# The samples' last rows in four column blocks on 128 partitions, and two row tiles weighted before their norm

## The chip, the cores and the metric

The kernel runs on one core of one Trainium2 chip. The metric is the device time of one execution in microseconds (us): the median of 3 runs of the kernel before is 829.52 us, with a lowest of 829.44 and a highest of 830.91. The profile is one execution more, recorded by the hardware profiler; its own time was 829.68 us.

## What is computed

One step of a hybrid decoder layer: a matrix-memory branch (mLSTM) and a sliding-window attention branch are merged by sigmoid gates into `u`; the output projection follows, scaled by a gate that depends on the conditions `c`, is added to the input, and a final RMS norm with the weight `g_final` ends the step. There are 1024 prompt rows and 8 x 4 = 32 sample rows, each of 1024 columns. The change touches only this end:

```
def rmsnorm(x, g):
    xf = x.astype(jnp.float32)
    y = xf * lax.rsqrt(jnp.mean(xf * xf, axis=-1, keepdims=True) + NORM_EPS)
    return (y * g.astype(jnp.float32)).astype(x.dtype)
...
    u = jax.nn.sigmoid(gm) * (y_m @ w_mo) + jax.nn.sigmoid(ga) * (y_a @ w_ao)
    x = x + gate * (u @ w_o)
...
    y_prompt = rmsnorm(yp, g_final)
    y_sample = rmsnorm(ys, g_final)
```

`u @ w_o` is a product of (1024 + 32) x 1024 by 1024 x 1024 in fp32.

## The kernel before

Everything lies in one function, `body`, which builds five instruction streams: TensorE (PE), VectorE (DVE), ScalarE (ACT), GpSimd (POOL) and the DMA queue of SyncE (SP). Each stream is executed strictly in the order in which it stands; what an instruction needs from another stream it waits for by a semaphore, and everything behind it in its own stream waits too. A scheduler makes the streams out of the program's calls: with `V.on`, `S.on` and `G.on` (line 2214) the calls on DVE, ACT and POOL from there on keep the order of the program text, PE always keeps it (`mm`, line 271), but DMAs on SP (`issue`, line 260) are placed by the scheduler, unless `late` (or a call that is `paced`) ties them behind others.

Two stages matter here.

**`mem_out(d, ...)`**, the last stage before the output rows (d = 0 to 7, the loop at line 2109). PE makes the 12-product pieces named `g_w_mo`; for each piece DVE multiplies the finished accumulator into a gate tile `tgw_mo` that SP has loaded from DRAM, and POOL (for d = 6 and 7) adds that to `u_l`, the second half of `u`. The first factor of the products, `ym_h` and `ym_l`, lies in the two memory blocks "l0" and "h0" (line 1714). The accumulators of d = 7 are in the PSUM banks that the output rows use next, so the banks come free when DVE has multiplied them out.

**The output rows** (loop at line 2219). The 1024 prompt rows go in four blocks of 256 rows, `r` = `blocks_of_rows[i]`. One block is a 2 x 2 block product by seven products (`r.product(1..7)`) over the first half of the inner dimension, and plain products (`r.plain`) over the second half, each in three passes (high x high, high x low, low x high parts). The accumulators are X, Z, W and Y (`foX`, `foZ`, `foW`, `foY` in the profile). ACT copies an accumulator on (`copied`: W becomes a copy of X, Y a copy of W) and PE then goes on adding to the original, so PE waits for those copies. ACT also splits `u` into parts for the next products (tiles `u0whC`, `u0whD` and so on), and DVE subtracts to make the low parts. In the first block ACT and DVE still split the last raw weights `wop` that SP loads (`wo_p0h`, `wo_p1h`). A row tile of 128 rows is finished in these steps: DVE adds the accumulator to the residual (`add_row`), ACT squares it with a running sum (`square`, tile `sq`), DVE and ACT make the inverse root (`norm_rows`: tiles `fv`, `fw`, `fy`; ACT does the square root), DVE multiplies by it and by `g_final` (`rows_out`, one `SCALAR_TENSOR_TENSOR` for each half of 512 columns), and SP stores it.

The tiles of this stage are eight row tiles `misc[0..7]` of 128 x 1024 (`rows_l` is 0 to 3, `rows_h` 4 to 7), which lie on the two blocks "l0" and "h0" (line 2128). So no DMA may fill any of them before the last `g_w_mo` product has read `ym_l` and `ym_h`.

The **sample rows** (`sample_rows`, a generator that `aside` moves on by a step at given places) are made beside this: 16 fp32 products of 32 x 512, four at a time in the four 32-column groups of PE (`fo`), each group holding the sum over other inner tiles; so ACT and DVE add four 32-row pieces for each half, then gate, residual, two squares of 32 x 512 and two multiplications of 32 x 512 follow in the last block.

In the last block (i = 3, `nxt` is None) `norm_rows` handles three columns: row tiles 4 and 5 of the block before and the samples; then `rows_out(4)` and `rows_out(5)` (the "fifth and sixth row tile") are four DVE multiplications.

Of the kernel before, what the change touches and what calls it, by code (L numbers as in the profile page):

```python
# [10 lines left out]
F32 = mybir.dt.float32  # L11
# [9 lines left out]
D = 1024  # L21
SEQ = 1024
# [151 lines left out]
def body(tc, a):  # L174
    nc = tc.nc
    with ExitStack() as ctx:
# [1760 lines left out]

        gbD, gsD = dp.tile([1, D], F32, name="gbD"), dp.tile([NS, D], F32, name="gsD")

        def ada_gate():  # L1940
            for j in range(2):
                cj = slice(j * 512, (j + 1) * 512)
                raws = []
                for k in range(KT):
                    raws.append(ht([128, 512], f"adar_ga{j}{k}"))
                    dma(raws[-1], a["w_ada"][4 + j, :, k])
                    yield 2.0, ""
                gb = ht([128, 512], f"gb{j}")[:9]
                dma(gb, a["b_gate"][:, cj].to_broadcast((9, 512)))
                yield 5.0, "b"  # L1950
                acc = pb([128, 512], f"ada_ga{j}")
                yield from ada_products(raws, acc)
                for r in range(0, 128, 32):
                    V.tensor_tensor(gb, acc[r:r + 9], gb, op=ALU.add)
                V.tensor_scalar(gb, gb, 0.25, None, op0=ALU.mult)
                dma(gbD[:, cj], gb[0:1])
                for t in range(NT):
                    dma(gsD.rearrange("(b t) e -> b t e", t=NT)[:, t, cj], gb[1:9])
                yield 3.0, "b" if j == 0 else ""
            dma(c32, hD[:, :, SEQ:T])  # L1960
# [168 lines left out]
        misc = [t[:, i] for t in rows for i in range(4)]  # L2129
        gsb, gf = misc[0], misc[2]  # L2130
        dma(gf, a["g_final"].to_broadcast((128, D)), True)
        S.activation(gf, gf, AF.Copy, scale=-1.0)
        dma(gsb[:NS], gsD, True)

        def residual(tb, n):
            xb = misc[3 + tb % 4 if tb < 8 else 7]
            dma(xb[:n], a["x_prompt"][tb * 128:tb * 128 + 128] if tb < 8 else a["x_sample"], tb < 4)
            return xb
# [18 lines left out]
        def rows_out(tb, xb, r, by=V):  # L2157
            yo, n = (a["y_p"][tb * 128:tb * 128 + 128], 128) if tb < 8 else (a["y_s"], NS)
            for c, eng in zip(HALF[::-1], (by, V)):
                if eng is S:  # L2160
                    S.activation(xb[:n, c], xb[:n, c], AF.Copy, scale=r[:n])
                else:
                    V.scalar_tensor_tensor(xb[:n, c], xb[:n, c], r[:n], gf[:n, c], op0=ALU.mult, op1=ALU.mult)
                issue(yo[:, c], xb[:n, c], eng=nc.scalar if eng is S else None)

# [3 lines left out]
        def sample_rows():  # L2169
            raws = [misc[m][:, c] for m in (1, 7) for c in HALF]  # L2170
            acc = [po([128, 512], f"fo8_{f}") for f in range(2)]
            sums = []

            def load(f, kq):
                for j in range(4):
                    dma(raws[j], a["w_out"][(kq + j) * 128:(kq + j + 1) * 128, HALF[f]], f == kq == 0)

            def products(f, kq):
                for j in range(4):
                    mm(acc[f][32 * j:32 * j + 32], u(kq + j, SEQ, NS), raws[j], start=(kq == 0), stop=(kq > 0), share=4)  # L2180

            load(0, 0)
            yield
            for f in range(2):
                products(f, 0)
                load(f, 4)
                yield
                products(f, 4)
                sums.append(raw_tile("fo8s").rearrange("p k n -> p (k n)")[:NS])
                S.copy(sums[f], acc[f][0:32])  # L2190
                if f == 0:
                    load(1, 0)
                else:
                    xb = residual(8, NS)
                yield
                for j in (32, 64, 96):
                    V.tensor_tensor(sums[f], acc[f][j:j + 32], sums[f], op=ALU.add)
                yield
            for f in range(2):
                V.tensor_tensor(sums[f], sums[f], gsb[:NS, HALF[f]], op=ALU.mult)  # L2200
                V.tensor_tensor(xb[:NS, HALF[f]], xb[:NS, HALF[f]], sums[f], op=ALU.add)
            row8.append(xb)

        row8 = []

# [9 lines left out]
        lo, hi = HALF  # L2215
        dma(gsb[:NS], gsD)
        blocks_of_rows[0].start("p1")
        xb = ss = None
        for i, r in enumerate(blocks_of_rows):
            nxt = blocks_of_rows[i + 1] if i < 3 else None  # L2220
            aside = lambda *when: next(rows8, None) if i in when else None
            before, xb, ss = (xb, ss), [residual(2 * i + c, 128) for c in range(2)], sm([128, 6], "fss", 2)
            aside(0)
            X, Z = pg([128, 512], "foX"), pa([128, 512], "foZ")
            r.product(1, X, True)
            W = copied(X, "foW", pg, new=r if i == 0 else None)
            if i:
# [4 lines left out]
            if i:  # L2232
                square(before[0][0][:, hi], before[1][:, 1:2])
                square(before[0][1][:, lo], before[1][:, 2:3])
                if i == 3:
                    V.memset(before[1][:, 4:6], 1.0)
                    for c in range(2):
                        square(row8[0][:NS, HALF[c]], before[1][:NS, 4 + c:5 + c])
                rs = norm_rows(before[1], 2 if nxt else 3, 2)
            if not nxt:  # L2240
                for c in range(2):
                    rows_out(4 + c, before[0][c], rs[:, c:c + 1])
            r.product(2, X, False)
# [26 lines left out]
            if nxt:  # L2270
                seventh()
                nxt.start(5)
                aside(1, 2)
                r.plain(1, 1, Z, range(2, 4))
# [10 lines left out]
            else:  # L2285
                rows_out(8, row8[0], rs[:, 2:3])
                first_row()
                seventh()
                square(xb[0][:, hi], ss[:, 1:2])
# [5 lines left out]
                for f, (y, (c0, n)) in enumerate(zip(Y, parts)):  # L2295
# [3 lines left out]
                    if f:  # L2299
                        V.tensor_tensor(xb[1][:, hi], xb[1][:, hi], gf[:, hi], op=ALU.mult)  # L2300
                        half = norm_sum(ss[:, 2:4], 1, 2)
# [9 lines left out]
OUTS = {  # L2311
    "y_p": (SEQ, D), "y_s": (NS, D), "C_p": (NH, 128, 128), "n_p": (128, NH), "m_p": (1, NH),
    "k_p": (128, 128), "v_p": (128, 128), "C_s": (NH, 128, NB, 128), "n_s": (128, NH, NB), "m_s": (NH, NB),
# [4 lines left out]
def lay_out(i):  # L2318
# [15 lines left out]
                                 xt[:, :, SEQ:].reshape(128, -1), np.zeros((128, 512 - C_TRI - 28 - KT * (9 + NS)), np.float32)], 1),  # L2334
        "x_prompt": np.asarray(i["x_prompt"])[0], "x_sample": np.asarray(i["x_sample"]).reshape(NS, D),
        "b_gate": np.asarray(i["b_ada"])[:, 2 * D:],
# [30 lines left out]
def unpack(r):  # L2367
    kv = lambda t: np.ascontiguousarray(t.transpose(1, 0, 2)).reshape(1, NB, 128, 2, 64)
    f = np.ascontiguousarray
    return (  # L2370
        r["y_p"].reshape(1, SEQ, D), r["y_s"].reshape(NB, NT, D),
        r["C_p"].reshape(1, 1, NH, 128, 128), f(r["n_p"].T).reshape(1, 1, NH, 128), r["m_p"].reshape(1, 1, NH),
# [11 lines left out]
```

## Time and profile before

| What | Value |
|---|---|
| median of 3 runs | 829.52 us |
| the profiled execution, its own time | 829.68 us |
| its span, first to last instruction | 827.9 us |
| ACT busy | 419.0 us (51%) |
| DVE busy | 590.5 us (71%) |
| DMA, mean over the span | 186 GB/s |
| output rows, first PE product to last instruction | 733.09 to 827.9 us |

The profiled execution's time is 1.8 us more than its span. Times in the views are us from the start of the span. In a timeline row the first number is the start, the second the time from there to the end of the instruction (or of the merged group, whose count stands behind the x); in brackets stands the idle time of that engine before it and what ended it. Instructions of one engine overlap a little, since the next starts before the last has drained. SPq rows are the SP queue's own: the time is that of issuing a DMA, and where rows are merged, the waits between them are in it.

### The profile page before, as it was taken

To read this page: it belongs to the slowest core of one execution; us is meant where nothing else is said; L and a number is where in the kernel's file an instruction comes from. 1 tells how busy PE (TensorE), PEld (TensorE's weight loads), DVE (VectorE), ACT (ScalarE), POOL (GpSimd) and SP (SyncE) were. 2 spreads that over 40 slices of the span, in tenths; PEclk is the share of its full clock that TensorE was granted. 3 is DMA by queue.
4 is the path that set the end of the run, shared out by engine and by line. 5 is a ranking of instruction groups with operands and counts; after the bars stand their busy time and mean duration, and the time that the engine had idled before them with its cause. 6 is when DMAs were issued, how large, how long until landed. Compare 5 with 4: busy or idle time off the path is not lost.

```text
span 827.9 us, 15032 instructions
## 1 busy us (share of the span) xinstructions
PE 810.2 (98%) x5129; PEld 670.4 (81%) x5129; DVE 590.5 (71%) x1479; ACT 419.0 (51%) x1030; POOL 67.2 (8%) x128
## 2 busy tenths in 40 slices
PE   6999999999999999999999999999999999999996
PEld 3779897888787888888888878888888789987775
DVE  4899886746646456475667886897669988864776
ACT  5664365556455564545455454544446654344343
POOL 0120000000000001000001010000002104250000
PEclk9999999999999999999999999999999999999998
DMA  9994757456535415538867444454446685643532
GB/s 335 377 341 137 225 183 233 140 163 195 176 124 187 140 65 168 177 124 270 262 209 255 159 136 137 139 180 160 136 127 202 217 298 172 202 153 116 202 109 108
DMA packets 106689, 153.95 MB, mean 186 GB/s; under 512 B 20449, under 2 KB 54369, under 8 KB 106581
## 3 DMA queue, kind: packets, MB, share of 16 engines
q1 hardware_dynamic: 100964, 142.25, 52.4%
q10 hardware_dynamic: 4176, 6.56, 2.2%
q0 software_dynamic: 1472, 4.20, 1.3%
q8 instruction: 40, 0.66, 0.3%
q14 instruction: 37, 0.30, 0.1%
HBM read 109.22 MB, written 44.75 MB: 186 GB/s over the span
## 4 chain that ended last, share of the span: by engine, by line
PE 87%; DMA 4%; issue 4%; DVE 2%; ACT 1%; SPq 1%; DVEq 0%; POOLq 0%; POOL 0%
PE bx L275 10%; PE bw L275 10%; PE by L275 10%; PE g_aq L275 6%; PE g_w_mo L275 6%; PE bz L275 5%; PE foW L275 3%; PE foX L275 3%; PE foY L275 2%; PE smp L275 2%; PE g_mq L275 2%; PE foZ L275 2%; PE sc L275 2%; PE oT L275 2%; PE pt L280 2%
## 5 line engine op out<-in xcount | busy, mean ns | idle before, releaser
L220 ACT ACTIVATE p<-p,nmx 128x256 f32<-128x256 f32 (+1 forms) x64 | 31.0, 486 | 18.7 <-DVE nmx L220 18.4
L275 PE MATMUL g_aq<-h_h,wh_aq 128*128 128x384 f32 (+1 forms) x96 | 32.3, 336 | 0.0
L275 PE MATMUL g_aq<-h_h,wl_aq 128*128 128x384 f32 (+1 forms) x96 | 30.9, 322 | 0.0
L275 PE MATMUL g_aq<-h_l,wh_aq 128*128 128x384 f32 (+1 forms) x96 | 30.9, 322 | 0.0
L275 PE MATMUL g_w_mo<-ym_h,wh_w_mo 128*128 128x384 f32 (+1 forms) x96 | 30.8, 321 | 0.0
L275 PE MATMUL g_w_mo<-ym_l,wh_w_mo 128*128 128x384 f32 (+1 forms) x96 | 30.8, 321 | 0.0
L275 PE MATMUL g_w_mo<-ym_l,wl_w_mo 128*128 128x384 f32 (+1 forms) x96 | 30.8, 321 | 0.0
L220 DVE CUSTOM_DVE_ANT_0 p<-sc,cst,sink 128x256 f32<-128x256 f32 (+1 forms) x64 | 26.1, 463 | 5.3 <-PE sc L275 5.2
L261 POOL DMA_DIRECT2D oD<-uqv x16 | 8.8, 552 | 183.7 <-ACT uqv L220 163.8
L275 PEld LDWEIGHTS g_aq<-h_h,wh_aq 128*128 128x128 f32 x96 | 18.0, 188 | 2.6 <-issue 1.5
L275 PEld LDWEIGHTS g_w_mo<-ym_l,wh_w_mo 128*128 128x128 f32 x96 | 18.0, 188 | 0.0
L275 PE MATMUL sc<-ukv,uqv 64*128 64x256 f32 (+1 forms) x128 | 18.0, 390 | 0.1
L275 PEld LDWEIGHTS g_aq<-h_l,wh_aq 128*128 128x128 f32 x96 | 18.1, 188 | 0.0
L275 PEld LDWEIGHTS g_w_mo<-ym_h,wh_w_mo 128*128 128x128 f32 x96 | 18.0, 188 | 0.0
L275 PEld LDWEIGHTS g_aq<-h_h,wl_aq 128*128 128x128 f32 x96 | 18.0, 188 | 0.0
L275 PEld LDWEIGHTS g_w_mo<-ym_l,wl_w_mo 128*128 128x128 f32 x96 | 18.0, 188 | 0.0
L220 DVE COPY p<-pt 128x512 f32<-128x512 f32 (+1 forms) x16 | 10.5, 655 | 10.3 <-PE pt L280 10.3
L220 DVE TENSOR_TENSOR et<-et,S 128x384 f32<-128x384 f32 (+1 forms) x12 | 6.1, 509 | 16.1 <-PE S L275 13.4
L275 PE MATMUL g_mq<-h_h,wh_mq 128*128 128x384 f32 (+1 forms) x48 | 16.8, 350 | 0.3 <-ACT mk L220 0.3
L220 ACT ACTIVATE sq<-rows_h 128x512 f32<-128x512 f32 (+2 forms) x14 | 8.2, 583 | 17.7 <-issue 12.0
L280 PE MATMUL pt<-cst,p 128*128 128x128 f32 x120 | 16.4, 277 | 0.5 <-DVE mx L220 0.5
L220 ACT ACTIVATE p<-p,den 128x256 f32<-128x256 f32 (+1 forms) x32 | 14.2, 490 | 3.7 <-DVE den L220 3.7
(2073 smaller groups left out, 2840.6 us busy)
## 6 DMA issues: line engine op xcount, KB each, us to landing
x<-xT SPq DMA_DIRECT2D x16, 256.0 KB
early_h<-w_ada SPq DMA_DIRECT2D x8, 512.0 KB
adar_ga<-w_ada SPq DMA_DIRECT2D x16, 256.0 KB
wr_ga<-w SPq DMA_DIRECT2D x16, 256.0 KB
wr_gm<-w SPq DMA_DIRECT2D x16, 256.0 KB
taD<-gt SPq DMA_DIRECT2D x16, 256.0 KB
tmD<-gt SPq DMA_DIRECT2D x16, 256.0 KB
wor<-w_out SPq DMA_DIRECT2D x16, 256.0 KB
```

Source lines behind the costliest of these rows:

```text
L220: ins = f(*args, **kw)
L261: ins = (eng or nc.sync).dma_start(out, in_)
L275: in_order(nc.tensor.matmul(out, lhsT, rhs, start=start, stop=stop, skip_group_check=more))
L280: in_order(nc.tensor.transpose(out, in_, idn))
```

## The change

The sample rows are laid out anew. Before, a sample's 1024 columns were on one partition; now the 32 rows stand four times below each other, with 256 columns each (partition 32 j + row holds columns 256 j to 256 j + 255), so the gate `gsD`, the residual `x_sample`, the weight and the result `y_s` are 128 x 256. Each of PE's four column groups then makes another 256 columns over all inner tiles (32 products of 32 x 256), nothing is left to add over groups, and the samples need on DVE two additions or multiplications of 128 x 256, on ACT one square, and at the end one multiplication. The sum over the four blocks for the norm is made by four PE products of one column (`fo8s`). The samples' weight is loaded by four broadcast DMAs and negated by ACT in the first block.

For row tiles 4 and 5, DVE multiplies by `g_final` ahead of the norm (`weighted`), and ACT multiplies by the inverse root afterwards (`rows_out(..., None)`).

```
-        gbD, gsD = dp.tile([1, D], F32, name="gbD"), dp.tile([NS, D], F32, name="gsD")
+        gbD, gsD = dp.tile([1, D], F32, name="gbD"), dp.tile([4 * NS, D // 4], F32, name="gsD")
...
-        gsb, gf = misc[0], misc[2]
+        gf = misc[2]
+        gs8, gf8, x8, y8 = (misc[0][:, c:c + 256] for c in range(0, D, 256))
         dma(gf, a["g_final"].to_broadcast((128, D)), True)
         S.activation(gf, gf, AF.Copy, scale=-1.0)
-        dma(gsb[:NS], gsD, True)
...
         def rows_out(tb, xb, r, by=V):
+            yo = a["y_p"][tb * 128:tb * 128 + 128]
+            for c, eng in zip(HALF[::-1], (by, V if by is not None else S)):
+                if eng is V:
+                    V.scalar_tensor_tensor(xb[:, c], xb[:, c], r, gf[:, c], op0=ALU.mult, op1=ALU.mult)
                 else:
+                    S.activation(xb[:, c], xb[:, c], AF.Copy, scale=r)
+                issue(yo[:, c], xb[:, c], eng=nc.scalar if eng is S and by is S else None)
+
+        def weighted(xb, c):
+            V.tensor_tensor(xb[:, c], xb[:, c], gf[:, c], op=ALU.mult)
...
         def sample_rows():
             raws = [misc[m][:, c] for m in (1, 7) for c in HALF]
+            acc = po([128, 512], "fo8")[:, :256]
...
+            def products(q):
+                for n in range(8):
+                    k, j = 2 * q + n // 4, n % 4
+                    mm(acc[32 * j:32 * j + 32], u(k, SEQ, NS), raws[n // 2][:, 256 * (j % 2):256 * (j % 2) + 256], start=(k == 0), stop=(k == KT - 1), share=4)
...
+            products(3)
+            yield
+            V.tensor_tensor(gs8, acc, gs8, op=ALU.mult)
+            V.tensor_tensor(x8, x8, gs8, op=ALU.add)
+            square(x8, sq8)
...
         V.on = S.on = G.on = True
         lo, hi = HALF
-        dma(gsb[:NS], gsD)
...
             aside(0)
+            if not i:
+                dma(gs8, gsD)
+                for j in range(4):
+                    dma(gf8[32 * j:32 * j + 32], a["g_final"][:, 256 * j:256 * j + 256].to_broadcast((32, 256)))
+                S.activation(gf8, gf8, AF.Copy, scale=-1.0)
+                dma(x8, a["x_sample"])
             X, Z = pg([128, 512], "foX"), pa([128, 512], "foZ")
             r.product(1, X, True)
+            if i == 3:
+                sum8 = pb([128, 512], "fo8s")[:, :1]
+                for j in range(4):
+                    mm(sum8[32 * j:32 * j + 32], cst[:, C_S32:C_S32 + 32], sq8, start=True, stop=True, share=4)
             W = copied(X, "foW", pg, new=r if i == 0 else None)
...
                 if i == 3:
-                    V.memset(before[1][:, 4:6], 1.0)
-                    for c in range(2):
-                        square(row8[0][:NS, HALF[c]], before[1][:NS, 4 + c:5 + c])
+                    V.memset(before[1][:, 5:6], 0.0)
+                    V.tensor_copy(before[1][:, 4:5], sum8)
+                if not nxt:
+                    for c, x in ((lo, 0), (hi, 1), (hi, 0), (lo, 1)):
+                        weighted(before[0][x], c)
                 rs = norm_rows(before[1], 2 if nxt else 3, 2)
             if not nxt:
                 for c in range(2):
-                    rows_out(4 + c, before[0][c], rs[:, c:c + 1])
+                    rows_out(4 + c, before[0][c], rs[:, c:c + 1], None)
...
-                rows_out(8, row8[0], rs[:, 2:3])
                 first_row()
+                V.scalar_tensor_tensor(y8, x8, rs[:, 2:3], gf8, op0=ALU.mult, op1=ALU.mult)
+                issue(a["y_s"], y8)
```

The rows below are the built instruction streams, with the semaphores that a row waits for (PE, DVE, Activation and Pool are engines, DMAHW0 to 7 the landings of earlier DMAs).

The SP queue at the end of `mem_out`, before: `wop` are raw weights, `tgw_mo` with `tmD_166` the gate tiles of d = 7.

```order
L261 DMA wop_8511<-woDp_4703 128x512 [waits DMAHW5_49,Pool_49]
L261 DMA tgw_mo_0_8517<-tmD_166 128x384 [waits DMAHW6_49]
L261 DMA tgw_mo_1_8519<-tmD_166 128x384 [waits DMAHW7_49]
L261 DMA tgw_mo_2_8521<-tmD_166 128x288 [waits DMAHW0_49]
L261 DMA wop_8572<-woDp_4726 128x512 [waits DMAHW1_49,Pool_49]
L261 DMA wop_8578<-woDp_4791 128x512 [waits DMAHW3_49,DMAHW2_49,DVE_49]
L261 DMA wop_8584<-woDp_4815 128x512 [waits DMAHW5_49,DVE_49]
L261 DMA rows_l_8651<-g_final 128x1024 [waits DMAHW4_49,PE_49]
L261 DMA rows_l_8651<-gsD 32x1024
```

The SP queue there now:

```order
L261 DMA wop_8511<-woDp_4703 128x512 [waits DMAHW5_49,Pool_49]
L261 DMA rows_l_8651<-gsD 128x256 [waits DMAHW6_49,PE_49]
L261 DMA tgw_mo_0_8517<-tmD_166 128x384 [waits DMAHW7_49]
L261 DMA tgw_mo_1_8519<-tmD_166 128x384 [waits DMAHW0_49]
L261 DMA tgw_mo_2_8521<-tmD_166 128x288 [waits DMAHW1_49]
L261 DMA wop_8572<-woDp_4726 128x512 [waits DMAHW2_49,Pool_49]
L261 DMA rows_l_8651<-g_final 32x256 [waits DMAHW3_49]
L261 DMA rows_l_8651<-g_final 32x256 [waits DMAHW4_49]
L261 DMA rows_l_8651<-g_final 32x256 [waits DMAHW5_49]
L261 DMA rows_l_8651<-g_final 32x256 [waits DMAHW6_49]
L261 DMA rows_l_8651<-x_sample 128x256 [waits DMAHW7_49]
L261 DMA wop_8578<-woDp_4791 128x512 [waits DMAHW0_49,DVE_49]
```

The load of `gsD`, the first into a row tile and so the one that waits for PE's last `g_w_mo` product, has moved from behind all loads of this stage to ahead of the three gate tiles; five small loads more stand ahead of the last two `wop` loads.

ACT in the first block of the output rows, before:

```order
L220 CAST u0whC<-u_l_7572 128x512 [waits PE_49,Activation_49,Pool_49]
L220 COPY foW<-foX 128x512 [waits PE_49]
L220 CAST wo_p1h<-wop_8572 128x512 [waits DMAHW1_49]
L220 CAST wo_p0h<-wop_8578 128x512 [waits DMAHW2_49]
L220 CAST wo_p1h<-wop_8584 128x512 [waits DMAHW3_49]
L220 COPY fop_8687<-foZ 128x512 [waits PE_49]
```

ACT there now:

```order
L220 CAST u0whC<-u_l_7572 128x512 [waits PE_49,Activation_49,Pool_49]
L220 CAST wo_p1h<-wop_8572 128x512 [waits DMAHW2_49]
L220 ACTIVATE rows_l_8651<-rows_l_8651 128x256 [waits DMAHW5_49,DMAHW4_49,DMAHW6_49,DMAHW3_49,PE_49]
L220 COPY foW<-foX 128x512 [waits PE_49]
L220 CAST wo_p0h<-wop_8578 128x512 [waits DMAHW0_49]
L220 CAST wo_p1h<-wop_8584 128x512 [waits DMAHW1_49]
L220 COPY fop_8691<-foZ 128x512 [waits PE_49]
```

The sign change of the samples' weight (`rows_l` 128x256) waits for the four broadcast loads and stands ahead of the copy `foW<-foX`.

ACT in the last block, before: squares, square root, and the two copies of W that PE waits for.

```order
L220 ACTIVATE sq,fss<-rows_l_8651 128x512 [waits DVE_49,Activation_49]
L220 ACTIVATE sq,fss<-rows_h_8652 128x512 [waits DVE_49,Activation_49]
L220 ACTIVATE sq,fss<-rows_h_8652 32x512 [waits DMAHW1_49,DMAHW5_49,DVE_49,Activation_49]
L220 ACTIVATE sq,fss<-rows_h_8652 32x512 [waits DMAHW6_49,Activation_49]
L220 ACTIVATE fy<-fv 128x3 [waits DVE_49]
L220 COPY foY_9279<-foW 128x256 [waits PE_49]
L220 COPY foY_9281<-foW 128x256 [waits PE_49]
```

ACT there now:

```order
L220 ACTIVATE sq,fss<-rows_l_8651 128x512 [waits DVE_49,Activation_49]
L220 ACTIVATE sq,fss<-rows_h_8652 128x512 [waits DVE_49,Activation_49]
L220 ACTIVATE fy<-fv 128x3 [waits DVE_49]
L220 ACTIVATE rows_l_8651<-rows_l_8651,fy 128x512 [waits DVE_49]
L220 ACTIVATE rows_l_8651<-rows_l_8651,fy 128x512
L220 ACTIVATE rows_h_8652<-rows_h_8652,fy 128x512 x2
L220 COPY foY_9294<-foW 128x256 [waits PE_49]
L220 COPY foY_9296<-foW 128x256 [waits PE_49]
```

The two 32-row squares are gone, and four multiplications by the inverse root stand between the square root and the copies of W.

63 lines of the change are left out of this document (19 added, 44 removed).

## The prediction

> **What bounds the kernel now.** I read the page first, then the chain of waits over the last stages, then the timelines of the engines at the two places where the order of work changes.
>
> ```profile
> PE 810.2 (98%) x5129; PEld 670.4 (81%) x5129; DVE 590.5 (71%) x1479; ACT 419.0 (51%) x1030; POOL 67.2 (8%) x128
> ```
>
> PE is busy for 98% of the span. An average over stages says little about one of them, so the chain of waits from 700 us on (start, duration, what) comes next:
>
> ```profile
> 699.85 33.40 PE g_w_mo L275 x210
> 733.25 1.38 PE foX L275 x6
> 734.63 0.23 PE foW L275
> ...
> 750.08 0.99 PE fo L275 x8
> ...
> 813.61 1.45 PE foY L275 x12
> 815.06 0.02 issue
> 815.08 0.38 ACT foy L220
> ...
> 823.07 0.75 DVE rows_h L220
> ```
>
> From 700 to 815 us the chain is PE alone, without one wait. Only the last 8 us alternate between ACT and DVE. So before 815 us no work taken off DVE or ACT can gain anything, while every wait put on PE is paid in full. I therefore look for new waits of PE.
>
> **First place: the SP queue before the output rows (term A).**
>
> ```profile
> 709.39 1.37 SPq L261 DMA_DIRECT2D tgw_mo<-tmD  x3
> 710.86 0.38 SPq L261 DMA_DIRECT2D wr_w_mo<-w_mo  x1
> 715.88 2.46 SPq L261 DMA_DIRECT2D wop<-woDp  x3
> 718.38 1.38 SPq L261 DMA_DIRECT2D tgw_mo<-tmD  x3
> 715.41 0.62 ACT L220 CAST wh_w_mo<-wr_w_mo 128x512 fp32r<-128x512 f32 x1 [1.97 <-DMA wr_w_mo<-w_mo]
> 718.37 0.62 ACT L220 CAST wo_p0h<-wop 128x512 fp32r<-128x512 f32 x1 [2.03 <-DMA wop<-woDp]
> ```
>
> The three gate tiles of d = 7 are issued at 718.38, 15 us before they are used, 0.46 us apart. A load issued alone (715.88) is used 2.5 us later (718.37); one behind three others (710.86) is used 4.55 us later (715.41).
>
> In the changed order the load of `gsD` stands ahead of these gate tiles. It fills a row tile on the memory of `ym_l`, so it waits for the last `g_w_mo` product, which ends at 733.25 by the chain. Queued behind it on SP are the three gate tiles, a raw weight, the four broadcasts of the samples' weight and two more raw weights. They all now start from 733.3, the gate tiles instead of from 718: `gsD` 733.3, first gate tile 733.8, the raw weight 735.1, the broadcasts 735.6 to 737.0 (steps of 0.46).
>
> Who waits for them is seen in the same place before:
>
> ```profile
> 733.04 1.37 DVE L220 SCALAR_TENSOR_TENSOR tgw_mo<-tgw_mo,g_w_mo 128x384 f32<-128x384 f32 x3
> 734.71 0.62 ACT L220 CAST u0whC<-u_l 128x512 fp32r<-128x512 f32 x1 [3.00 <-POOL u_l L220]
> 735.23 0.58 ACT L220 COPY foW<-foX 128x512 f32<-128x512 f32 x1
> 735.75 0.61 ACT L220 CAST wo_p1h<-wop 128x512 fp32r<-128x512 f32 x1
> 736.07 0.39 PE L275 MATMUL foX<-wo_b21h,u0whB 128*128 128x512 f32 x1
> ```
>
> DVE's multiplication of the gate tile frees the PSUM banks that `foW` and `foZ` take, and starts the way over POOL to ACT's cast `u0whC` (733.04 to 734.71, 1.67 us). Behind this cast ACT now has the cast of the raw weight, the sign change of the samples' weight, and only then the copy of X to W. PE's product into X at 736.07 (`foX<-wo_b21h`) adds to what that copy reads, so it waits.
>
> The sum: the first gate tile is behind one small load, so I take 3.0 us, nearer to 2.5 than to 4.55: landed 736.8. The cast `u0whC` starts 1.67 later, 738.4. The next cast follows 0.52 later (735.23 to 735.75 is that step), the sign change another 0.52 later, 739.5. The last broadcast, issued at 737.0, lands 2.5 us later, also 739.5. The sign change has half of a cast's columns, 0.3; the copy takes 0.58; PE goes on at 740.4 instead of 736.07. **A = 4.3 us.** It is at least 3.8 (gate tile after 2.5 us and no wait for the broadcasts: 738.9 + 0.9) and at most 5.8 (gate tile after 4.55 us). The last raw weights come late too, but are first needed 3.4 us after that product starts, at 743.8, and land near 741; that cover holds up to about 2 us.
>
> The Trainium skill, "DMA: Bandwidth & Descriptors", section "Anatomy of one DMA", gives a DMA a fixed cost of about 2.0 us plus its bytes over 436 GB/s. That would be an estimate of 2.1 us for a broadcast and 2.45 for a gate tile, thus 3.9 instead of 4.3, and a sum 0.4 us lower. The 2.5 us of the row above for 256 KB agrees with the page's 2.6; I keep the rows.
>
> **Second place: the last block (term B).** The four DVE multiplications of row tiles 4 and 5 become four multiplications by `g_final` on DVE ahead of the norm, and four on ACT behind it.
>
> ```profile
> 802.63 0.59 ACT L220 COPY fop<-foZ 128x512 f32<-128x512 f32 x1 [0.79 <-PE foZ L275]
> 804.25 0.60 ACT L220 ACTIVATE sq<-rows_l 128x512 f32<-128x512 f32 x1
> 805.15 0.60 ACT L220 ACTIVATE sq<-rows_h 128x512 f32<-128x512 f32 x1 [0.18 <-DVE rows_h L220]
> 808.12 0.63 ACT L220 COPY foY<-foW 128x256 f32<-128x256 f32 x2
> 823.07 0.72 ACT L220 ACTIVATE rows_h<-rows_h,fy 128x512 f32<-128x512 f32 x1 [0.68 <-DVE fy L220]
> 801.75 0.67 DVE L220 TENSOR_TENSOR fo8s<-fo8s,rows_l 32x512 f32<-32x512 f32 x1
> 804.39 0.67 DVE L220 TENSOR_TENSOR rows_h<-rows_h,foY 128x512 f32<-128x512 f32 x1
> 805.59 0.74 DVE L220 TENSOR_TENSOR uwlE<-u_h,uwhE 128x256 fp32r<-128x256 f32 x2
> 807.81 0.16 DVE L220 SCALAR_TENSOR_TENSOR fv<-fss,fv 128x3 f32<-128x3 f32 x1 [0.44 <-ACT sq L220]
> 808.85 0.16 DVE L220 SCALAR_TENSOR_TENSOR fy<-fw,fy 128x3 f32<-128x3 f32 x1
> 820.14 0.68 DVE L220 TENSOR_TENSOR rows_h<-rows_h,rows_l 128x512 f32<-128x512 f32 x1
> 820.75 0.14 DVE L220 TENSOR_SCALAR fv<-fss 128x1 f32<-128x1 f32 x1
> 809.37 0.39 PE L275 MATMUL foW<-wo_b22h,uwhE 128*128 128x512 f32 x1
> ```
>
> Before, ACT's copies of W run from 808.12 to 808.75, and PE writes W again at 809.37: 0.6 us of slack. Now the copies stand behind the four scalings, and these behind the inverse root.
>
> When the root is ready: the four new one-column products stand before Z's products. No row shows four such products. The nearest, sixteen PE instructions of one column at the start, take 1.01 us (quoted below), so half as many about 0.5; bounds 0.2 and 1.0. Z's copy and the first square move with it, to 803.1 and 804.75. The second square no longer waits for DVE, because the four sample operations (801.75 to 804.39, 2.6 us) ahead of `rows_h<-foY` are gone; it follows at 805.4 and is read by 806.1. DVE has its two low parts when ACT's casts are done, about 805.3, takes 0.3 for the copy of the samples' sum, and starts weighting at 805.6. A multiplication of 128 x 512 takes 0.68, and 0.61 from its start to the next (820.14 to 820.75): four end at 808.1. The two `fv` and the root, 0.21 and 1.20 us (807.81 to 809.01), then give it at 809.5, against 809.01 before.
>
> A scaling on ACT is the row at 823.07, 0.72 us, some 0.1 less from start to start: four take 2.5, to 812.0. The two copies take 0.63. PE writes W at 812.7 instead of 809.37. **B = 3.3 us** with the four products in it; with their bounds, and 0.55 to 0.72 for a scaling, 2.7 to 4.1. What lies on ACT behind the copies is not late for itself: the tail from 815.06 on (the seventh product, its copy, the square, the norm, the last sums) hangs on PE and moves as a whole.
>
> **What costs nothing.** The sample products:
>
> ```profile
> 309.17 1.01 PE smp L275 x32
> 6.46 1.01 PE L275 MATMUL xc<-one,xsq 128*32 128x1 f32 x16 [6.46 <-ACT xsq L220]
> ```
>
> A set of four at 512 columns took 0.99 (`fo` x8 in the chain). Eight at 256 columns have the same columns in twice the instructions, and `smp`, again half as wide with 32 instructions, takes 1.01: nothing, or at most 0.1 for four sets. The lower DVE and ACT work in blocks two and three (sums, copies) is hidden: PE did not wait there. If that cover were gone, it would be a gain of at most the 0.3 us named below. The other pattern of the `gsD` stores lies far from any wait.
>
> The sum is 4.3 + 3.3 = 7.6 us on the profiled execution's 829.68, 837.3; that execution is 0.16 above the median of the runs, so **837.1 us**, with bounds of the terms 835.9 to 839.4.
>
> **The rivals.** *Clock.* Both places leave PE idle for nearly 3 us. The only such idle time in the trace is after the last product:
>
> ```profile
> 820.20:823.60 3.40, 0.54 (x5) 0.33 (x3) 2.85 (x12) 1.25 (x4) 0.00 (x0) 1.00 0.39 144
> ...
> 823.70:827.80 4.10, 0.00 (x0) 0.00 (x0) 0.12 (x1) 0.09 (x1) 0.00 (x0) 0.50 0.34 128
> ```
>
> In these windows (length, busy time of PE, PEld, DVE, ACT, POOL, then the granted clock, DMA share and rate) the clock is still whole up to 823.6 and a half after 823.7, some 2.9 us after PE's last product. The stall B is 2.8 us of complete idleness (809.9 to 812.7), A is broken by `foW` and Z's six products. If the clock fell in one of them and came back in the time that it took to fall, about 2.9 us at half speed would lose 1.5 us: 838.6 for one, 840.1 for both. Against it: the idle time is just short, and PE works a little within it. Chance 0.28. The Trainium skill, "TensorE: Matmul & The Clock Gate", Part 1, has the clock halved after an idle window of about 3.4 us and restored after a busy one as long; the windows run free of the kernel. By that rule neither stall need reach a whole idle window, yet the trace halves the clock after 2.9 us, so the rule does not exclude this rival; it would make the loss an estimated 1.7 us for each.
>
> *Only one stall.* If the gate tiles were not on PE's way (A none), 832.8; if the scalings were not (B only 0.5 for the four products), 834.3. For it: both stalls are worked out from the order of the queues, and an estimate of a start that is wrong by 2 us would melt one. Against it: the waits are in the built streams, and the two engines have nothing else to do then. Chance 0.13, evenly split.
>
> *The end gets shorter.* This is the other side:
>
> ```profile
> 820.46 0.28 PE L275 MATMUL foY<-wo_p0h,u3wlD 128*128 128x256 f32 x1
> 821.08 0.41 DVE L220 TENSOR_TENSOR rows_h<-rows_h,foY 128x256 f32<-128x256 f32 x1
> ```
>
> The last product ends at 820.74, but DVE takes its sum only at 821.08, since it is behind. DVE has four multiplications (2.7 us at 0.68) less behind the norm; if it were in time, 0.3 us would go, 829.2. It decides only if both stalls are under 0.3 us together. Chance 0.04, half of it within 0.2%.
>
> **How the numbers follow.** Both stalls at a whole clock: 0.55, 837.1 with its own range 835.9 to 839.4. Clock 0.28, one stall 0.13, shorter end 0.04. The range for 8 in 10 runs from 834.0 (leaving out the shorter end and the case without A) to 840.6 (leaving out a fall of the clock at both places on top of a long A). What a measurement can tell is about 0.2%, 1.7 us. All cases but the last are slower by more than 3 us: slower 0.96, within 0.2% 0.02, faster 0.02.
>
> **What would show it.** A: an SP row of `gsD` issued at about 733.3 with the `tgw_mo` rows behind it; idle PE before `foW`, before `foZ` and before `foX<-wo_b21h`, which starts near 740.4, and ACT's row `rows_l` 128x256 right ahead of the copy `foW`. B: idle PE of 2.8 us before `foW<-wo_b22h` (in the clock of before 812.7, with A 817), ended by ACT's copies `foY`, and four ACT rows with `fy` ahead of these. Sample products: four `fo` groups of about 1.0 us. Clock: a window with less than 1.00 before the last product. The forecast is wrong if PE has no idle time at one of the two places, or if the chain after the seventh product has changed in length by more than 0.3 us.

## The result

The changed kernel takes 839.89 us in the median of 6 runs (837.11 to 842.36), the kernel before 830.29 in 6 runs beside it (829.44 to 830.91): ratio 1.012, 95% interval 1.0098 to 1.0141. It is 9.6 us slower; 7.6 were forecast. The profiled execution was the lowest of the six, 837.11 us with a span of 835.3.

**The first place.** The chain of waits of the changed kernel from 727 us on (start, duration, what):

```profile
727.86 4.37 PE g_w_mo L275 x28
...
732.25 0.32 SPq L261
...
735.91 3.23 DMA rows_l<-g_final
...
739.24 0.42 ACT rows_l L220
739.66 0.49 ACT foW L220
...
740.20 4.38 PE foX L275 x18
```

Where PE stood alone before, the chain now leaves PE at 732.23, goes through the SP queue, the last broadcast of `g_final` and two ACT instructions, and comes back at 740.20. The SP queue's timeline there, with the gate tiles behind `gsD`:

```profile
732.25 0.32 SPq L261 DMA_DIRECT2D rows_l<-gsD  x1
732.62 1.38 SPq L261 DMA_DIRECT2D tgw_mo<-tmD  x3
734.09 0.38 SPq L261 DMA_DIRECT2D wop<-woDp  x1
734.51 1.82 SPq L261 DMA_DIRECT2D rows_l<-g_final  x4
```

ACT's timeline (the bracket is the engine's idle time before the row, and what ended it):

```profile
737.01 0.62 ACT L220 CAST u0whC<-u_l 128x512 fp32r<-128x512 f32 x1 [6.34 <-POOL u_l L220]
737.96 0.62 ACT L220 CAST wo_p1h<-wop 128x512 fp32r<-128x512 f32 x1 [0.33 <-DMA wop<-woDp]
739.24 0.42 ACT L220 ACTIVATE rows_l<-rows_l 128x256 f32<-128x256 f32 x1 [0.66 <-DMA rows_l<-g_final]
739.57 0.58 ACT L220 COPY foW<-foX 128x512 f32<-128x512 f32 x1
```

And PE's own rows in that stretch and at the start of the second block, then the same start before:

```profile
732.06 0.39 PE L275 MATMUL foX<-wo_b11h,u0whA 128*128 128x512 f32 x1
735.96 0.49 PE L275 MATMUL foW<-wo_b11h,u0whA 128*128 128x512 f32 x1 [2.36 <-DVE tgw_mo L220]
740.20 0.50 PE L275 MATMUL foX<-wo_b21h,u0whB 128*128 128x512 f32 x1 [0.76 <-ACT foW L220]
759.51 0.39 PE L275 MATMUL foX<-wo_b11h,u1whA 128*128 128x512 f32 x1
```

```profile
733.09 0.39 PE L275 MATMUL foX<-wo_b11h,u0whA 128*128 128x512 f32 x1
755.23 0.39 PE L275 MATMUL foX<-wo_b11h,u1whA 128*128 128x512 f32 x1
```

From the first product of the output rows to `foX<-wo_b21h` it is 8.14 us, before 2.98 (736.07 - 733.09): 5.16 more. To the start of the second block it is 27.45 against 22.14: 5.31 more. Marks are compared as differences, since the stretch ahead of the output rows ends at another time in every profile (731.87 to 733.92 in those taken here).

**The second place.** The chain in the last block:

```profile
805.63 0.17 PE fo8s L275 x8
805.80 1.60 PE foZ L275 x6
...
809.94 0.67 DVE rows_l L220
...
813.57 0.17 DVE fy L220
...
813.76 1.33 ACT rows_l L220 x2
815.10 1.22 ACT rows_h L220 x2
816.32 0.54 ACT foY L220 x2
...
816.90 4.41 PE foW L275 x18
```

The four scalings stand between the root (813.57 + 0.17) and the copies of W (816.32), and PE waits for the copies. PE's rows show the same, first the changed kernel's two, then the start of that block before:

```profile
804.11 0.39 PE L275 MATMUL foX<-wo_b11h,u3whA 128*128 128x512 f32 x1
816.90 0.50 PE L275 MATMUL foW<-wo_b22h,uwhE 128*128 128x512 f32 x1 [2.55 <-ACT foY L220]
```

```profile
799.71 0.39 PE L275 MATMUL foX<-wo_b11h,u3whA 128*128 128x512 f32 x1
```

From the first product of the last block (804.11) to `foW<-wo_b22h` (816.90) it is 12.79 us, before 9.66 (809.37 - 799.71): 3.13 more. Of this 0.42 is not a wait: the one-column products take 0.17, and the six products into Z behind them 1.60 instead of 1.36.

**The rest.** A set of eight sample products (`fo`) takes 1.00 us where a set of four took 0.99; the stretch from the second block to the last (759.51 to 804.11) is 0.12 us longer than before (755.23 to 799.71). From `foW<-wo_b22h` to the end of the span it is 18.4 us, 0.1 less than before. Together 5.31 + 0.12 + 3.13 - 0.13 = 8.4 us. The profiled execution, which came to the output rows 1.03 us earlier than the one before, fits this: 829.68 - 1.03 + 8.4 = 837.1. The medians are 9.6 us apart. So 1.2 us are left that this one profile doesn't account for.

**The clock.** The granted clock fell in it, though. In the windows view (stretch, length, busy time of PE, PEld, DVE, ACT, POOL, granted clock, DMA share and rate), cut within 0.1 us of where the clock changes:

```profile
733.07:736.47 3.40, 1.02 (x4) 0.28 (x2) 1.05 (x2) 0.00 (x0) 0.49 (x1) 1.00 0.78 234
736.49:739.89 3.40, 2.90 (x6) 1.82 (x6) 1.28 (x2) 1.88 (x4) 3.40 (x4) 0.51 0.79 232
814.99:818.40 3.41, 1.50 (x7) 1.24 (x8) 0.43 (x1) 2.83 (x8) 0.00 (x0) 1.00 0.83 308
```

The changes lie on a grid of 3.41 us: at 736.55 and 739.95 in this profile; in that of e12 below at 736.6, 740.0, 818.6 and 822.0, and from the first to the third of these it is 24 times 3.41. After a window in which PE worked 1.02 us, the next ran at a half. It held Z's six products, behind which PE waited for ACT anyway, so here it cost nothing. After the window of the second stall, with 1.50 us of work, the clock stayed whole.

### The profile page after: what moved, and what is told of

Same layout as the page of the kernel before. It is cut to its first block, busy times and chain, and to the rows that moved or that the text cites. A ratio compares the mean times of both kernels' runs of the same rounds, so it can differ in the third digit from the quotient of the medians.

```text
span 835.3 us, 15099 instructions
## 1 busy us (share of the span) xinstructions
PE 812.4 (97%) x5169; PEld 671.4 (80%) x5169; DVE 582.1 (70%) x1471; ACT 419.9 (50%) x1031; POOL 66.7 (8%) x128
## 5 line engine op out<-in xcount | busy, mean ns | idle before, releaser
L220 ACT ACTIVATE p<-p,nmx 128x256 f32<-128x256 f32 (+1 forms) x64 | 31.0, 486 | 18.7 <-DVE nmx L220 18.4
L220 DVE SCALAR_TENSOR_TENSOR tgw_mo<-tgw_mo,g_w_mo 128x384 f32<-128x384 f32 (+1 forms) x24 | 12.3, 516 | 9.1 <-PE g_w_mo L275 5.0
L220 DVE COPY p<-pt 128x512 f32<-128x512 f32 (+1 forms) x16 | 10.5, 656 | 10.3 <-PE pt L280 10.3
```

The source lines that it names most:

```text
L220: ins = f(*args, **kw)
```

## The experiments

The first theory: two waits of PE, made by the place of the samples' loads on SP and of their sign change on ACT (A), and of the four scalings on ACT (B), plus what the half clock takes where it meets products that nothing hides. Ratios are to the kernel before, run beside it on the same chip.

### Both parts undone one by one

**The samples' loads a block later (e1_loads_later).**

```
-            if not i:
-                dma(gs8, gsD)
+            if i == 1:
+                dma(gs8, gsD, True)
...
-                dma(x8, a["x_sample"])
+                dma(x8, a["x_sample"], True)
```

(The four broadcasts are `late` too; the sign change stays between them.)

> The gate, weight and residual of the samples are loaded a block of rows later, behind that block's other loads, and the sign change goes with them; the last block stays as in the change. Theory: the first stall is gone, PE reaches foX<-wo_b21h 2.98 us after the first foX product as before (changed: 8.14), and the second stall of 3.0 us is all that is left: 833.3, up to 1.7 more in the runs where a window at half clock follows the stall. Rival (the late loads are not the cause, the 5 us come from the run-to-run place of the DMAs): the wait before foX<-wo_b21h stays, 837 to 840.

Measured: 838.92 us (838.57 to 839.55), ratio 1.0117, interval 1.0103 to 1.013. The time missed the expectation. PE's timeline tells why, in the second block:

```profile
754.75 0.39 PE L275 MATMUL foX<-wo_b11h,u1whA 128*128 128x512 f32 x1
761.06 0.50 PE L275 MATMUL foX<-wo_b21h,u1whB 128*128 128x512 f32 x1 [3.43 <-ACT foW L220]
783.02 0.39 PE L275 MATMUL foX<-wo_b11h,u2whA 128*128 128x512 f32 x1
```

In the first block the wait is gone, as expected: `foX<-wo_b21h` comes 2.97 us after the first product. But the sign change came along and now holds back the copy `foW` of the second block: 6.31 us instead of 2.72. Its four broadcasts are again issued just ahead of it, now behind that block's own loads; the last one lands 4.86 us after its issue (755.14 to 760.00). The whole block takes 28.27 us, 5.4 more than before (778.08 - 755.23 = 22.85): 3.6 for the wait, 0.1 as in the other blocks, and 1.7 for the clock:

```profile
758.52:761.93 3.41, 0.87 (x4) 0.74 (x5) 0.00 (x0) 1.83 (x4) 0.00 (x0) 1.00 0.09 24
761.94:765.34 3.40, 3.40 (x11) 2.66 (x10) 1.69 (x5) 3.37 (x9) 0.00 (x0) 0.55 0.00 0
```

The clock changes at 762.3 and 765.7, 0.4 us behind the cuts of these two rows, hence the 0.55; in the 3.41 us up to 762.3 PE works 1.27 us. Here the half window lies behind the wait, on products that nothing hides: 3.41 us at half speed, 1.7 lost. A second one, from 816.9 to 820.3, follows the stall of the last block: from `foW<-wo_b22h` to the end it is 19.7 us instead of 18.4. So the wait follows the sign change, wherever this stands close behind its loads and ahead of a copy that PE waits for.

**The loads a block later, the sign change two (e8_second_stall_alone).** As e1, with the sign change under `if i == 2:`.

> The loads of gate, weight and residual of the samples come a block later, the sign change two blocks later; the last block as in the change. Theory: PE has no wait in blocks one to three, and one in the last of 2.55 us, 12.63 us from the first foX product to foW<-wo_b22h: 829.5 + 3.0 = 832.5 in runs where the clock stays whole, 833.7 to 834.2 where a half window follows; so the runs should fall in this range, with a median near 833.3. Rival (no clock): 832.5 with the spread of before. Rival (the loads shift the wait on again, as they did when the sign change came only one block later): a wait before foX in block three, 837 or more.

Measured: 832.23 us (831.89 to 834.12), ratio 1.0035, interval 1.0022 to 1.0048. Its profile has one wait of PE in the output rows:

```profile
799.76 0.39 PE L275 MATMUL foX<-wo_b11h,u3whA 128*128 128x512 f32 x1
812.55 0.50 PE L275 MATMUL foW<-wo_b22h,uwhE 128*128 128x512 f32 x1 [2.55 <-ACT foY L220]
```

12.79 us, as in the changed kernel. Against the kernel before beside it (829.56) 2.7 us are left, near B's 3.13. The four lower runs have a mean clock of 0.998 or 0.999, the highest, 834.12, has 0.996; so the clock took its share in one run of five, and the median lies 1.1 us below the 833.3 that were expected. The loads and the sign change no longer cost anything.

**The sign change alone a block later (e4_sign_later).**

```
-                S.activation(gf8, gf8, AF.Copy, scale=-1.0)
                 dma(x8, a["x_sample"])
+            if i == 1:
+                S.activation(gf8, gf8, AF.Copy, scale=-1.0)
```

> Only the sign change of the samples' weight goes a block later; all loads stay where the change has them. Theory (the first stall is two waits: the late gate tiles, then the last broadcast): the gate tile's wait stays. ACT's copy foW follows the cast u0whC at once, so PE could reach foX<-wo_b21h 6.1 to 6.3 us after the first foX product (2.98 before, 7.7 to 8.2 changed) if Z's six products run at a whole clock, and 7.2 if these run at a half; so 3.2 to 4.2 us of the first stall stay, and with 3.0 for the second it is 835.6 to 838.5. Rival (the broadcasts are the whole stall): 2.98 us again, 832.4 to 834. Rival (the gate tiles are the whole stall): nothing changes, 839.

Measured: 837.41 us (836.43 to 838.26), ratio 1.0093, interval 1.008 to 1.0106: the middle case, the gate tiles' wait stays. `foX<-wo_b21h` comes 6.18 us after the first product, 3.20 more than before, as worked out. But the second block starts as late as in the changed kernel (27.32 us after the first product, 22.14 before). The next late load takes the saving; the chain has it:

```profile
739.17 7.10 DMA rows_l<-g_final
746.29 0.02 ACT rows_l L220
...
747.64 0.49 ACT foY L220
748.18 1.66 PE foY L275 x6
```

This is the broadcast of the prompt rows' weight (128 x 1024), which SP issues behind all the others, and whose sign change stands ahead of the copy `foY`. It landed 7.1 us after its issue. A half window (738.65 to 742.1) also slowed PE on its way there, but it is hidden: PE still had to wait for this copy. In the first profile of the changed kernel the same load took 5.8 us (738.40 to 744.22), and ACT was done with it before PE came to this point; in that of e0 it took 7.0 and was only just in time. So a stall that ends earlier runs into this load.

**Row tiles five and six by DVE again (e2_dve_rows).**

```
-                if not nxt:
-                    for c, x in ((lo, 0), (hi, 1), (hi, 0), (lo, 1)):
-                        weighted(before[0][x], c)
...
-                    rows_out(4 + c, before[0][c], rs[:, c:c + 1], None)
+                    rows_out(4 + c, before[0][c], rs[:, c:c + 1])
```

> Row tiles five and six are weighted and scaled in one on DVE again; all else as in the change. Theory: PE's second wait is gone but for the one-column products (0.2 us), the first stays with 5.2 us: 835.6, up to 1.7 more where the half clock outlasts the stall. Rival (the second stall is set by the one-column products and the norm with the samples' sum, not by ACT's scalings): the wait before foW<-wo_b22h in the last block stays near 2.5 us, 838 or more.

Measured: 834.56 us (834.39 to 835.92), ratio 1.0068, interval 1.0055 to 1.008, 5.1 us above before. `foW<-wo_b22h` comes 10.08 us after the block's first product, with no wait: 0.42 more than before. The first stall is there in full (8.20 us to `foX<-wo_b21h`).

**The scalings behind the copies (e5_copies_first).** The loop over `rows_out(4 + c, ...)` moved from behind the norm to behind `Y = [copied(W, ...)]`.

> The four scalings by ACT go behind its two copies of W; weighting on DVE ahead of the norm and all else as in the change. Theory (the second stall is ACT's queue): the copies now start after the square root, near 9.0 us after the first foX product of the last block, while PE's products ahead of foW<-wo_b22h last 10.1 us; no idle time there, only 0.4 us for the one-column products and the first foZ product behind them: 829.5 + 5.0 + 0.4 = 834.9, as with the DVE rows (834.56). Rival (the weighting ahead of the norm holds the copies up): 1 us or more of idle time stays, 836 or more.

Measured: 834.52 us (833.14 to 836.99), ratio 1.0065, interval 1.005 to 1.008; again 10.08 us and no wait. ACT's timeline:

```profile
812.55 0.21 ACT L220 ACTIVATE fy<-fv 128x3 f32<-128x3 f32 x1 [2.19 <-DVE fv L220]
812.72 0.63 ACT L220 COPY foY<-foW 128x256 f32<-128x256 f32 x2
813.59 1.34 ACT L220 ACTIVATE rows_l<-rows_l,fy 128x512 f32<-128x512 f32 x2 [0.23 <-DVE fy L220]
```

The weighting on DVE still puts off the square root to 812.55, but the copies follow it at once and are done before PE's products ahead of W are (`foW<-wo_b22h` at 814.02). So B is the four scalings in the queue ahead of the copies, and not the weighting.

**Both repairs (e6_loads_later_copies_first).** e8 and e5 together.

> Both repairs: loads a block and sign change two blocks later, scalings behind the copies of W. Theory: no wait of PE is left; the one-column products cost 0.4 us, the rest is hidden: 829.9, no difference that can be measured, clock 0.997 to 0.999 as before. Rival (the end gets shorter, since DVE has less behind the norm): 829.2 or less. Rival (something else in the change costs PE time that the two stalls do not hold): 831.5 or more.

Measured: 829.47 us (828.82 to 830.1, 11 runs) against 829.56 (17 runs), ratio 0.9998, interval 0.999 to 1.0007: no difference. `foX<-wo_b21h` comes 2.97 us after the first product of the first block, `foW<-wo_b22h` 10.08 us after that of the last, both without a wait. The two places were the whole cost. The gains of the change are there, but small: `foW<-wo_b22h` to the end is 18.3 us instead of 18.5, against 0.42 for the one-column products and the Z products behind them. None of the kernels here beats the one before.

### The clock

The changed kernel itself ran twice more, beside the others (first e0_changed_again, beside e1 to e3):

> The changed kernel itself, a second time, as the measure for the runs beside it. Theory (two stalls and the clock): the two new waits of PE cost 5.2 and 3.0 us, 838.4 on the median before of 830.3; whatever is above that comes from windows in which the granted clock is a half, where they fall depends on the run, so the median is again 839 to 841 with a spread of 3 to 5 us, and a profile in which PE's products run at a whole clock all through would be near 838. Rival (no clock): the landing times of the loads of the first stall vary by some us; the spread is the same, and it shows as a longer idle time before foX<-wo_b21h.

Measured: 839.25 us (837.99 to 839.39) against 829.45: 9.8 more, ratio 1.012, interval 1.0105 to 1.0136. Its profile, the lowest run, again had its only half window where it was hidden. The waits were as in the first profile (7.77 and 12.79 us). The spread was 1.4 us, not the 3 to 5 that were expected. As this profile is of the lowest run, it doesn't show where the median's 1.4 us above the 8.4 come from; the profiles of e9, e10 and e11 below, each of the highest run of a kernel that differs only in products added on PE, do. In them the last broadcast landed after 3.39, 3.12 and 3.16 us, at most 0.6 above the shortest here (2.77, e3): the landing times don't vary by some us. Each of them has a half window on products.

**PE kept at work in both stalls (e3_pe_filled, and again e11_both_filled_again).** The same product is made again, each time from zero, so nothing changes but PE's time:

```
             r.product(1, X, True)
+            for _ in range(1 if i == 0 else 0):
+                r.product(1, X, True)
...
-                mm(t, new.w[1][0][:, 0], wo["b11"][0][0][:, c], start=True, stop=True)
+                for _ in range(12 if name == "foY256" else 1):
+                    mm(t, new.w[1][0][:, 0], wo["b11"][0][0][:, c], start=True, stop=True)
```

> The changed kernel with PE kept at work in its two stalls: in the first block of rows the first product into X is made twice (six products more, 1.4 us, each overwriting its like), and in the last block the one product that opens the second bank of Y is made twelve times (1.3 us more). Both fit within the idle time. Theory (clock): no window with less than half of its time at work is left, the clock stays whole up to the last product; the time goes down by about what the median has above the plain stalls, 838 to 838.8, with a spread under 2 us. Rival (no clock): 839.9 with the same spread of 5 us, or more by the 2.7 us of added work if the waits are not idle time at all.

> Both stalls filled, a second time. Theory (clock): 8.0 us above before as the first time, clock 0.998 in most runs, and 1.5 us below the changed kernel of the same call. Rival (the first time was chance): as the changed kernel.

Measured: 837.44 us (836.55 to 838.92), ratio 1.01, interval 1.0085 to 1.0114; the second time 837.15 (836.74 to 839.41), 1.0098, interval 1.0084 to 1.0112. Both are 8.0 us above before, 1.8 and 2.3 below the unfilled kernel beside them, though PE has 2.7 us more to do. The intervals of each pair overlap a little; taken together, the nine filled runs lie 8.3 us above before on the mean, the eight unfilled ones 9.8. That the clock would be whole in every run was wrong: the first time one run, 838.92, has a mean clock of 0.995 (the others 0.998), and the second time the profiled execution, with 839.41 the highest, still fell. The first stall has two parts, and the added products fill only the one before `foW`. In the part behind Z's products PE is idle for 2.12 us:

```profile
738.55:741.95 3.40, 1.28 (x6) 0.89 (x6) 0.61 (x2) 2.18 (x5) 2.43 (x3) 1.00 0.86 235
741.97:745.37 3.40, 3.40 (x10) 2.62 (x9) 1.89 (x3) 1.87 (x4) 1.29 (x1) 0.50 0.92 300
```

**One stall filled at a time (e9_first_filled, e10_second_filled), and the changed kernel a third time (e12_changed_third),** beside e11.

> The changed kernel with PE kept at work in the first stall alone (the first product into X made twice). Theory (clock): the half windows of the first stall lie for the most part under PE's wait for the copy foW, those of the second hit products that nothing hides; so filling the first alone gains little, 7.9 to 9.5 us above before against 8.2 plain. Rival (the loss is in the first stall): 8.2 or less, as with both filled.

> The changed kernel with PE kept at work in the second stall alone (the product that opens the second bank of Y made twelve times). Theory (clock): most of what the changed kernel has above the plain 8.2 us is lost behind the second stall; with it filled the runs lie 7.5 to 8.8 us above before. Rival (no clock): as the changed kernel beside it, 9.5.

> The changed kernel a third time, beside the filled ones. Theory (clock): 9.5 us above before, with runs from 8 (clock whole where PE has work) to 12 (two half windows that hit products). Rival (no clock): the same as the filled kernels.

Measured against 829.18: first filled 838.31 (836.44 to 840.54, interval 1.0085 to 1.0122), second filled 838.38 (837.66 to 840.53, 1.0099 to 1.0134), none 839.45 (837.86 to 840.34, 1.0107 to 1.0138). The unfilled kernel is 10.3 above before, each single filling about 1.1 lower. With these intervals neither can be told from the other, nor for certain from the unfilled kernel; that the second stall holds most of the loss was not borne out. The windows of the unfilled one show both halves of the matter:

```profile
733.16:736.57 3.41, 1.10 (x6) 0.59 (x4) 0.65 (x2) 0.00 (x0) 0.02 (x1) 1.00 0.68 202
736.59:739.98 3.39, 3.39 (x7) 1.99 (x7) 1.62 (x3) 1.77 (x4) 3.39 (x4) 0.51 0.82 246
815.08:818.49 3.41, 1.41 (x6) 1.19 (x7) 0.42 (x1) 2.92 (x8) 0.00 (x0) 1.00 0.82 308
818.51:821.91 3.40, 3.40 (x10) 2.67 (x9) 0.00 (x0) 0.00 (x0) 0.00 (x0) 0.51 0.00 0
```

The first half window is hidden once more. The second meets the last block's products: from `foW<-wo_b22h` (817.08) to the end of the span (837.1) it is 20.0 us, where the profiles of the changed kernel without a half window there have 18.4. In e9 the same place took 20.1. In e10 it was the first stall: two half windows in a row, and the second block 6.88 us late instead of 5.31.

## Why the prediction was right, and where not

The forecast was 7.6 us on top of before; measured were 9.6. The median of 839.9 lies within the range of 834.0 to 840.6, but just above what the main case, both stalls at a whole clock, gave for itself (835.9 to 839.4; the lower end adds up to 836.0). The account: A 5.3 for 4.3, B 3.1 for 3.3, the middle blocks with the sample products 0.1 for 0, the end 0.1 shorter; the 1.2 that are left are put down to the clock, for which the main case had 0. That the profiled execution came out at 837.11, on the forecast's 837.1, is partly luck: it reached the output rows 1.03 us early, and its half window was hidden.

**What bounds the kernel: right.** The repaired kernel e6, with less work on DVE and no wait of PE, takes the time of before.

**Term A: right in its mechanism, mis-sized in one step.** `gsD` was issued at the end of the last `g_w_mo` product, the gate tile was used 2.73 us after its issue (3.0 taken: 732.62, then this row of DVE),

```profile
735.35 1.05 DVE L220 SCALAR_TENSOR_TENSOR tgw_mo<-tgw_mo,g_w_mo 128x384 f32<-128x384 f32 x2 [3.27 <-DMA tgw_mo<-tmD]
```

the cast `u0whC` came 1.66 later (1.67 taken), the last broadcast was issued 3.66 us after `gsD` (3.7 taken), and from the sign change to PE it took 0.96 (0.9 taken). What was wrong is the step "lands 2.5 us later" of the last broadcast: 3.23 us in this profile, and 2.77 to 3.39 in those of e0, e2, e3, e5 and e9 to e12. The row that it was taken from is of a load issued alone; this one had eight issued in the 3.7 us ahead of it. The prediction had 4.55 us for a load behind three others, took it as the bound for the gate tile, and gave the broadcast none. A filled queue makes plain loads late too: the raw weight issued at 734.09 landed just before the cast that waited for it started at 737.96, 3.87 us later. What the broadcast form adds, no run here separates. The forecast had the casts and the broadcast done at the same time, 739.5 on its scale; in the run ACT was through with the casts 0.66 us before the sign change could start. So the broadcast alone set the end of the stall, as e4 shows from the other side: without it `foX<-wo_b21h` came 3.20 us late instead of 5.16. The formula of the Trainium skill, "DMA: Bandwidth & Descriptors", section "Anatomy of one DMA", would have put the landing at an estimated 2.1 us, further off; the page has it for DMAs on the GpSimd path, while these go through SP, and the measurement decides.

**Term B: right.** 2.71 us of wait (2.55 in the view's own count) and 0.42 of products, 3.13, for 3.3 with 0.5 in it; it was the same 12.79 us in each of the ten profiles with the scalings ahead of the copies. e5 and e2 both take all of it but the 0.42 away.

**What costs nothing: right** within 0.12 us for the two middle blocks.

**The rival "clock": part of the truth, and set too low.** The forecast's chance of 0.28 rested on the idle time being just short of 2.9 us, and on PE's bit of work in between. Both arguments fall: the clock goes by windows of 3.41 us that lie anywhere, and a window with PE at work up to 1.5 us was enough. The prediction's own row at 820.20 had 0.54 us of PE's work in the window ahead of the fall, so the 2.9 us behind the last product were no length that a stall had to reach. Nor was this the only long idle time in the trace: the row that it quotes at 6.46 has 6.46 us of it at the start, at a clock that the view gives as whole; why it is shown as whole there stays open. The price, 1.5 us for each fall, was near: 1.6 to 1.7 where the half window lay wholly on products. It was paid in some runs, at one place or both, and nothing where the half window lay in the wait. On the median 1.2 to 1.9 us are left for it in the three measurements (9.6, 9.8 and 10.3 less 8.4), and it is part of the spread of 837 to 842. The Trainium skill, "TensorE: Matmul & The Clock Gate", Part 1, has the window and its free phase right (3.41 us here). It speaks of an idle window, while here windows of which PE worked 25 to 43% sufficed (0.85 us in e9, 815.87 to 819.27, and 1.48 in e12, 815.16 to 818.56, cut at the changes themselves).

**The rivals "only one stall" and "the end gets shorter": no.** Both stalls came. The end did get shorter, by 0.1 us, and by 0.25 where nothing waits (e6), close to the 0.3 that were named; it never decides.

## What to carry to other kernels

Before moving a load, ask what in the queue stands behind it, and for how long its own wait holds them all; here one small load that waited for a product, and four more that a sign change waited for, cost 5 us, because three gate tiles stood behind the first and a copy for PE behind the sign change. Where one engine carries the whole chain, an instruction on another engine that nobody waits for must still stand behind the ones that this engine waits for: the same four scalings cost 2.7 us ahead of two copies and nothing behind them. A stall of 2 to 3 us costs up to 1.7 us more by the clock, in a part of the runs, so such a cost is read from several runs and not from one profile.

## What the hardware showed beyond this

- The granted clock changes on a grid of 3.41 us whose place differs from run to run. Two almost equal windows, cut at the changes, decided differently: after 1.58 us of work in one (e4, 735.24 to 738.64) the clock was a half, after 1.57 us in the other (first profile, 815.06 to 818.47) it stayed whole. So the busy time as the profile models it isn't exactly what decides.
- A window at half clock in which PE has 2.2 us of work can be followed by another (e10, both behind the first stall):

```profile
735.35:738.75 3.40, 1.11 (x4) 0.67 (x4) 1.07 (x2) 0.05 (x1) 1.09 (x2) 0.99 0.83 265
738.77:742.17 3.40, 2.22 (x6) 1.21 (x5) 1.16 (x2) 2.07 (x4) 3.29 (x3) 0.50 0.78 255
742.18:745.58 3.40, 3.40 (x9) 2.62 (x10) 1.41 (x2) 2.54 (x5) 1.28 (x1) 0.51 0.73 208
```

- Loads land late in a filled queue: broadcasts of 32 x 256 in 2.8 to 3.4 us in the first block and 4.9 in e1, that of 128 x 1024 in 5.8 (first profile) to 7.6 (e9), a plain one of 128 x 512 in 3.9 (first profile), against 2.5 us for the latter issued alone before.
- Why the stretch ahead of the output rows ends up to 2 us apart from profile to profile stays open.
